# A first load of y on ScalarE's DMA queue, issued beside SyncE's first load of x

## The chip, the cores and the metric

The kernel runs on one core of one Trainium2 chip. The metric is the time of one execution on the device, in microseconds (us), lower is better. Ratios are the mean time of one kernel's runs over that of the other's in the same rounds, so they are not quite the ratio of the medians quoted beside them. Each series of experiments ran beside the kernel before on a chip of its own. The span is the part of an execution that the profile shows; it is 1.4 to 1.9 us shorter than the time. A packet is here one record of a DMA engine, one contiguous run of bytes; a transfer lands when its semaphore shows that all of it has arrived.

## The reference

```python
x, y: float32 [1024, 4096]
z = x + y
out = 0.5 * z * (1 + tanh(sqrt(2 / pi) * (z + 0.044715 * z**3)))   # float32
```

So 2 x 16.78 MB are read and 16.78 MB are written: 50.33 MB.

## The kernel before

Each of the 128 partitions holds 32,768 columns, in 16 chunks of 2,048. x is loaded in two transfers (16,384 columns, 65,536 B a partition), y in four (y0 to y3, 32,768 B a partition) into two buffers, and the result leaves in three stores. SyncE issues all of them on its one queue.

```python
    xloads = [16384, 16384]
    yloads = [8192, 8192, 8192, 8192]
    FIRST = 8
    stores = [16384, 10240, 6144]
...
    by_dve = {0: 0, 2: 0, 4: 2, 6: 4, 8: 8, 12: 10}   # add of chunk k by VectorE, ahead of its end(value)
...
    def add(c):      # z = x + y: VectorE for the chunks in by_dve, GpSimd for the other ten
        eng = nc.vector if c in by_dve else nc.gpsimd
        eng.tensor_add(out=zt[:, a:b], in0=zt[:, a:b], in1=yt[s][:, o : o + b - a])
    def mag(c):      # ScalarE: w = |z|, into PSUM
        nc.scalar.activation(out=wt[c], in_=zt[:, a:b], func=act.Abs)
    def gelu(c):     # ScalarE: w = gelu(-w), in PSUM
        nc.scalar.activation(out=wt[c], in_=wt[c], func=act.Gelu_apprx_tanh, scale=-1.0)
    def end(c):      # VectorE: z = max(z, 0) + w   (chunk 8, FIRST, in two halves)
        nc.vector.scalar_tensor_tensor(out=zt[..], in0=zt[..], scalar=0.0,
                                       in1=wt[c][..], op0=alu.max, op1=alu.add)
...
    # SyncE's queue: x(0), y0, y1, x(1), y2, y3, then the three stores;
    # y2 waits until y0's buffer is free; the first store waits for chunk FIRST
```

After compilation `begin_early(nc, 2)` moves SyncE's first two issues (x and y0) ahead of the barrier at which all engines start (1.26 us for ScalarE's table load in the timeline below). (The last function, `wait_late`, leaves the wait for the last store to ScalarE at the very end, and isn't touched.)

## Time and profile before

| | before |
|---|---|
| time, median of 3 runs (lowest to highest) | 120.17 us (120.11 to 120.28) |
| span of the profiled run | 118.8 us |
| busy: VectorE, ScalarE, GpSimd | 50%, 51%, 47% |
| the DMA queue's packets, share of 16 engines | 98.5% |
| mean rate over the span | 424 GB/s |

The way to read it: a share of half for each compute engine and of nearly all for the DMA engines says where the bound is, and the rate with the compute engines idle (437 GB/s from 3 to 15 us) and busy (437 GB/s from 31.6 to 70 us) says whether the transfers slow down when they work. The prediction below shows the lines. One pair of rows of GpSimd in the timeline (columns: start, length, engine, line, operation, shapes, and in brackets the idle time before it and what ended that) becomes important later. It is that of its first two adds of the second half:

```profile
70.53 6.62 POOL L149 TENSOR_TENSOR z<-z,y 128x2048 f32<-128x2048 f32 x1 [14.56 <-DMA y<-in_y_dram]
...
77.10 4.52 POOL L149 TENSOR_TENSOR z<-z,y 128x2048 f32<-128x2048 f32 x1
```

The same add takes 4.52 us once and 6.62 us once. The longer one began less than 0.05 us after an add of VectorE that took 2.29 us (its row stands in the prediction, at 70.48).

### The profile page before, as it was taken

The numbers are of one execution on the slowest core, as the hardware profiler recorded it, in microseconds if no ns is written. First come the engines' busy times: TensorE is split into PE (matmuls) and PEld (weight loads), VectorE is DVE, ScalarE is ACT, GpSimd is POOL, SyncE is SP. The second block draws the span as 40 slices with busy tenths as digits, with TensorE's granted clock in tenths as the row PEclk, the third lists the DMA queues.
The fourth block names the chain that finished last, engine by engine and source line by source line (L and its number), as shares of the span: only waits on it lengthen the run. The fifth ranks groups of instructions, "written<-read, shape, count | busy, mean of one in ns | idle before, by whom it ended". The sixth has DMA issues, their size and how long they took to land.

```text
span 118.8 us, 160 instructions
## 1 busy us (share of the span) xinstructions
DVE 59.8 (50%) x24; ACT 60.8 (51%) x34; POOL 55.5 (47%) x14
## 2 busy tenths in 40 slices
DVE  0000000000399999699994595257999457742000
ACT  5000000000057989999369804797798999940000
POOL 0000000000399999998000029999999999200000
DMA  9899988989999988998899999998899889999895
GB/s 353 353 419 596 397 353 364 497 375 463 419 430 452 530 353 375 640 397 353 353 463 419 452 430 397 474 541 353 375 640 397 353 353 441 441 441 441 381 422 257
DMA packets 1296, 50.33 MB, mean 424 GB/s; under 512 B 144, under 2 KB 144, under 8 KB 144
## 3 DMA queue, kind: packets, MB, share of 16 engines
q1 hardware_dynamic: 1296, 50.33, 98.5%
HBM read 33.55 MB, written 16.78 MB: 424 GB/s over the span
## 4 chain that ended last, share of the span: by engine, by line
DMA 48%; POOL 33%; POOLq 4%; ACT 3%; DVE 2%; issue 0%; SPq 0%; DVEq 0%
DMA y<-in_y_dram 48%; POOL z L149 33%; POOLq L215 4%; DVE z L166 2%; ACT w L154 2%; ACT w L157 2%; SPq L125 0%; POOLq L149 0%; DVEq L166 0%
## 5 line engine op out<-in xcount | busy, mean ns | idle before, releaser
L149 POOL TENSOR_TENSOR z<-z,y 128x2048 f32<-128x2048 f32 x10 | 55.3, 5560 | 45.9 <-DMA y<-in_y_dram 45.9
L154 ACT ACTIVATE w<-z 128x2048 f32<-128x2048 f32 x16 | 30.1, 1880 | 42.8 <-DVE z L149 36.3
L166 DVE SCALAR_TENSOR_TENSOR z<-z,w 128x2048 f32<-128x2048 f32 (+1 forms) x17 | 36.3, 2156 | 16.0 <-ACT w L157 16.0
L149 DVE TENSOR_TENSOR z<-z,y 128x2048 f32<-128x2048 f32 x6 | 24.0, 4009 | 30.6 <-DMA y<-in_y_dram 30.6
L157 ACT ACTIVATE w<-w 128x2048 f32<-128x2048 f32 x16 | 29.8, 1862 | 0.5
L200 ACT ACT_TABLE_LOAD x1 | 1.3, 1283 | 1.3 <-PEq L232 1.3
L199 DVE MEMSET one<- 128x1 f32 x1 | 0.1, 59 | 1.3 <-PEq L232 1.3
L200 ACT ACTIVATE one<-one 128x1 f32<-128x1 f32 x1 | 0.2, 203 | 0.0
L232 POOL MEMSET const-float32-0.0<- 128x1 f32 x1 | 0.1, 99 | 0.2 <-issue 0.2
L232 POOL MEMSET const-bfloat16-1.0<- 128x1 bf16 x1 | 0.1, 102 | 0.0
L232 POOL MEMSET const-uint8-127<- 128x1 uint8 x1 | 0.1, 102 | 0.0
L232 POOL MEMSET const-float32-1.0<- 128x1 f32 x1 | 0.1, 99 | 0.0
## 6 DMA issues: line engine op xcount, KB each, us to landing
y<-in_y_dram SPq DMA_DIRECT2D x4, 4096.0 KB, 28.3
out_dram<-z SPq DMA_DIRECT2D x1, 5120.0 KB, 14.9
out_dram<-z SPq DMA_DIRECT2D x1, 3072.0 KB, 10.9
z<-in_x_dram SPq DMA_DIRECT2D x2, 40.5
out_dram<-z SPq DMA_DIRECT2D x1, 21.6
```

What stands on the lines that cost most here:

```text
L149: eng.tensor_add(out=zt[:, a:b], in0=zt[:, a:b], in1=yt[s][:, o : o + b - a])
L154: nc.scalar.activation(out=wt[c], in_=zt[:, a:b], func=act.Abs)
L157: nc.scalar.activation(out=wt[c], in_=wt[c], func=act.Gelu_apprx_tanh, scale=-1.0)
L166: ins = nc.vector.scalar_tensor_tensor(out=zt[:, a + o : a + o + n], in0=zt[:, a + o : a + o + n], scalar=0.0, in1=wt[c][:, o : o + n], op ...
L199: nc.vector.memset(one, 0.0)
L200: nc.scalar.activation(out=one, in_=one, func=act.Gelu_apprx_tanh)
L215: tc.compile()
L232: nc = _bacc.Bacc("TRN2", target_bir_lowering=False, num_devices=1)
```

## The change

The intent: y0 need not stand behind x in SyncE's queue. ScalarE has a queue of its own and nothing to do at the start (its first row in the timeline before, the table load, comes at 1.26 us), so it issues y0 as its very first instruction, while SyncE issues x.

```diff
-def begin_early(nc, count):
+def begin_early(nc):
     head, body = (b.instructions for b in nc.main_func.blocks[:2])
-    SP = mybir.EngineType.SP
-    moved = [i for i in body if i.engine == SP and isinstance(i, mybir.InstDMACopy)][:count]
-    ...
+    for engine in (mybir.EngineType.SP, mybir.EngineType.Activation):
+        first = next(
+            i for i in body if i.engine == engine and isinstance(i, mybir.InstDMACopy)
+        )
+        ...
+        body.remove(first)
+        head.insert(next(k for k, i in enumerate(head) if i.engine == engine), first)
...
-        nc.sync.dma_start(out=yt[s][:, o : o + b - a], in_=yv[:, a:b])
+        eng = nc.sync if i else nc.scalar
+        eng.dma_start(out=yt[s][:, o : o + b - a], in_=yv[:, a:b])
...
-    begin_early(nc, 2)
+    begin_early(nc)
```

More of the change, by code (lines that the diff above doesn't have):

```diff
@@ L6 @@
 from concourse._compat import with_exitstack
-def begin_early(nc, count):
+def begin_early(nc):
     head, body = (b.instructions for b in nc.main_func.blocks[:2])
-    SP = mybir.EngineType.SP
-    moved = [i for i in body if i.engine == SP and isinstance(i, mybir.InstDMACopy)][:count]
-    assert not any(i.sync_info and i.sync_info.on_wait for i in moved)
-    assert all(i.regs_accessed() == ((), ()) for i in moved)
-    at = next(k for k, i in enumerate(head) if i.engine == SP)
-    for k, i in enumerate(moved):
-        body.remove(i)
-        head.insert(at + k, i)
+    for engine in (mybir.EngineType.SP, mybir.EngineType.Activation):
+        first = next(
+            i for i in body if i.engine == engine and isinstance(i, mybir.InstDMACopy)
+        )
+        assert not (first.sync_info and first.sync_info.on_wait)
+        assert first.regs_accessed() == ((), ())
+        body.remove(first)
+        head.insert(next(k for k, i in enumerate(head) if i.engine == engine), first)
 def wait_late(nc):
```

## The prediction

> **What bounds the kernel now.** I read the page's head first, then its DMA part, then windows of the trace, then SyncE's timeline. The page:
>
> ```profile
> span 118.8 us, 160 instructions
> ...
> DVE 59.8 (50%) x24; ACT 60.8 (51%) x34; POOL 55.5 (47%) x14
> ...
> DMA packets 1296, 50.33 MB, mean 424 GB/s; under 512 B 144, under 2 KB 144, under 8 KB 144
> ...
> q1 hardware_dynamic: 1296, 50.33, 98.5%
> ```
>
> No compute engine is busy much more than half of the span, but the one DMA queue's packets fill 98.5% of the time of 16 DMA engines. Is that a full rate, or slow packets? The windows view (columns: stretch, length, busy DVE, ACT and POOL, clock, DMA share, GB/s) answers:
>
> ```profile
> 3.00:15.00 12.00, 0.00 (x0) 0.00 (x0) 0.00 (x0) 1.00 1.01 437
> 31.60:70.00 38.40, 34.19 (x12) 29.57 (x16) 24.22 (x4) 1.00 1.01 437
> 85.00:105.00 20.00, 14.50 (x6) 18.57 (x11) 16.59 (x4) 1.00 0.97 422
> ```
>
> The rate is the same with idle compute engines (3 to 15) and busy ones (31.6 to 70). A packet counts where it starts, so such a window is good to some per cent. Sharper: in the trace's packet records a 65,536 B packet takes 2.418 us at the median, and each engine starts its next packet as the last one ends, with no gap over 0.06 us from its first packet to its last. So 16 engines move 16 x 65,536 / 2.418 = 433.7 GB/s, and 50.33 MB need 50,330 / 433.7 = **116.05 us** at the least. The span of 118.8 leaves 2.75 us that is not steady streaming, and only that can shrink. Where it lies, at the front:
>
> ```profile
> 0.00 0.38 SPq L125 DMA_DIRECT2D z<-in_x_dram  x1
> 0.23 0.10 POOL L232 MEMSET const-float32-0.0<- 128x1 f32 x1 [0.23 <-issue]
> ...
> 0.43 1.16 SPq L132 DMA_DIRECT2D y<-in_y_dram  x2
> 1.26 1.28 ACT L200 ACT_TABLE_LOAD   x1 [1.26 <-PEq L232]
> ```
>
> SyncE's first issue (x, columns 0 to 16383) is over at 0.38; the second (y0) starts at 0.43, so the new version can advance y0 by about 0.4 us and no more. The third (y1, merged into the same row) comes after the starting barrier. The packet records have the first data packet at 1.01 us, the sixteenth engine's first at 1.52 us, and those first packets last 2.6 to 3.5 us in place of 2.42. At the end the last packet is over at 118.34 and the last semaphore comes at 118.75. The engine that began at 1.15 us with a 3.50 us packet sums up well: 1.15 + (3.50 - 2.42) + 116.05 + 0.4 = 118.7.
>
> The page's chain of waits names compute after the loads (POOL 33%), but that is a chain of releases; the stores' issue times show its slack:
>
> ```profile
> 77.86 0.35 SPq L136 DMA_DIRECT2D out_dram<-z  x1
> ...
> 96.59 0.34 SPq L136 DMA_DIRECT2D out_dram<-z  x1
> ...
> 107.81 0.33 SPq L136 DMA_DIRECT2D out_dram<-z  x1
> ```
>
> The last y load lands at 80.1 (semaphore records), the first store at 99.4, the second at 111.5. An issue takes 1.0 us to its first packet (as at the front), and a landing shows some 0.4 us after its last packet (as at the end). So a store may come 1.4 us before the earlier landing without a gap: the three stores have 0.8, 1.4 and 2.3 us to spare on the engine that is last. Compute isn't the bound, but has only about 1 us in hand at the first store.
>
> [...]
>
> **The change part by part.** The bytes, tiles, sums and stores stay as they are. A comparison of the instruction order confirms that SyncE loses one DMA issue, ScalarE gains one ahead of everything else, and VectorE and GpSimd keep their order.
> - *Removed:* 0.42 us of SyncE's queue. Work waits on the DMA engines, which have about 19 us of x ahead of them, not on the issue. Gain: 0.
> - *Barrier earlier:* it needs SyncE, now free at about 0.4 us in place of 0.85; ScalarE's own issue of about 0.4 us takes that up in part. The table load and y1's issue come perhaps 0.3 us earlier; ScalarE's first real work is at 34.0 us, y1's data at about 31. Gain: 0.
> - *Moved:* x and y0 now share the engines from 1 us on. The first sum needs both, that is 8.39 + 4.19 = 12.58 MB in either order: 12,580 / 433.7 = 29.0 us plus the start, the 31.6 at which y0 lands now. x should land near 31 in place of 21.9 and nothing asks for it sooner. Gain: 0.
> - *First packet:* x is issued as before, so 1.01 us stays. An engine whose first x packet comes late (1.52) might start on y0's first. I choose a gain of 0.1 us out of the 0.5 us spread, a guess.
> - *Tail:* the same stores on the same queue. 0.
>
> Sum: 120.17 - 0.1 = **120.07**, written 120.1.
>
> **The rivals.**
> 1. *Overlapped queues shorten the start.* First packets take about 0.7 us more than steady ones; if that is latency of one queue's first read, a second queue could fill it. For: the excess is there. Against: both begin at the same moment, and neither is warm. It would make 119.4. One in eight.
> 2. *Switching costs.* Each engine turns between 8 packets of x and 8 of y0, some 16 switches. With 0.05 us lost in each, 0.8 us are added, and all of it reaches the end, as the engines have no slack: 121.0. To pass 2% (2.4 us), 0.15 us a switch is needed. Against: in the old trace neighbouring packets join without gaps even where x ends and y0 begins; but that is one queue. One in eight, beyond 2% one in thirty.
> 3. *y1 slips in front of y0's end.* y1 now stands behind x on SyncE's queue, not behind y0. If y0 lags by a packet, one y1 packet (1.21 us) goes first, y0 lands at 32.8 and VectorE's eight chunks finish that much later. Two rows of the old timeline carry the slack:
>
> ```profile
> 67.91 2.29 DVE L166 SCALAR_TENSOR_TENSOR z<-z,w 128x2048 f32<-128x2048 f32 x1 [1.46 <-ACT w L157]
> 70.48 2.29 DVE L149 TENSOR_TENSOR z<-z,y 128x2048 f32<-128x2048 f32 x1 [0.29 <-DMA y<-in_y_dram]
> ```
>
> VectorE ends its first half at 70.20 and waits 0.29 us for y2. Of 1.2 us, 0.3 vanish there and 0.8 in the first store's slack, so about 0.1 us is left: 120.2. Likely in part (one in three), and almost free.
> 4. *The issue holds x up.* [...] One in six.
>
> **Range and chances.** Most ways end between 119.9 and 120.5, the rivals at 119.4 and 121.0. The range 119.5 to 120.9 leaves one in ten on either side. Faster by 2% would be 117.8; without any start or end cost the span would be 116.05 and the time, 1.4 us longer than the span as now, 117.4. Almost all of the overhead would have to go: 1%. Slower by 2% needs rival 2 at its strongest: 3%. The rest, 96%, is within.
>
> **What would show it.** In the new profile: two data queues, together again near 98.5%; x landing at about 31 us, within 2 us of y0; the first VectorE sum at 31.3 to 32.9; stores at about 78, 96.6 and 107.8; 65,536 B packets alone at 2.42 us after the first load. If x lands near 22 and y0 near 31, the queues don't share. If the first sum starts after 33 us while y1 has not gained, switching costs. If the first packet comes before 0.9 us, the start is shortened, and rival 1 or an earlier ScalarE did it. The prediction is wrong if the steady packet time changes while two queues run, or if a gap of over 0.5 us opens ahead of the first store.

The fourth rival: by the length of one issue (0.38 us for x, 0.42 for y0), that rival put x up to 0.4 us late, at 120.5. That the steady part has nothing to give rests on the rate alone (437 GB/s with compute idle and busy, packets of 2.418 us without gaps); that no faster packets are possible is the assumption. That the engines take turns between two queues, which "Moved" and the second and third rival build on, was at that time an assumption as well; the packet records of the changed kernel show it, below.

## The result, and the profile after

The changed kernel took 120.30 us (median of 6 runs, 120.15 to 120.52), the kernel before 120.22 us (6 runs). The ratio is 1.0007, with a 95% interval of 0.9995 to 1.002: the same.

The page of the changed kernel has two data queues where there was one:

```profile
span 119.0 us, 160 instructions
...
DMA packets 1296, 50.33 MB, mean 423 GB/s; under 512 B 144, under 2 KB 144, under 8 KB 144
...
q1 hardware_dynamic: 1152, 46.14, 90.6%
q10 hardware_dynamic: 144, 4.19, 8.2%
```

Together they fill 98.8% of the engines' time: as full as before, with the same packets and bytes. The start of the timeline:

```profile
0.00 0.39 SPq L125 DMA_DIRECT2D z<-in_x_dram  x1
0.12 0.37 ACTq L133 DMA_DIRECT2D y<-in_y_dram  x1
...
0.91 1.28 ACT L201 ACT_TABLE_LOAD   x1 [0.91 <-PEq L233]
0.91 0.33 SPq L133 DMA_DIRECT2D y<-in_y_dram  x1
```

ScalarE issues y0 at 0.12 us, 0.31 us earlier than SyncE did, and does so while SyncE issues x; neither takes longer than alone (0.39 us for x and 0.37 for y0, against 0.38 and 0.42 one after the other in the kernel before). The barrier is over 0.35 us sooner (the table load begins at 0.91 in place of 1.26). Then nothing follows from it. The packet records show the first packet of x at 1.02 us and the first of y0 at 3.93 us: each engine first finishes a packet of x. The landings show what was traded:

| landing, us | before | changed | changed, second trace |
|---|---|---|---|
| x, first load | 21.91 | 31.60 | 31.56 |
| y0 | 31.61 | 31.76 | 31.74 |
| y1 | 41.33 | 41.33 | 41.29 |
| y2 | 70.39 | 70.63 | 70.35 |
| last store | 118.75 | 119.00 | 118.71 |

x lands 9.7 us later and y0 within 0.15 us of where it did. As the first sum needs both, it starts within 0.16 us of where it did (31.70 before):

```profile
31.86 2.29 DVE L150 TENSOR_TENSOR z<-z,y 128x2048 f32<-128x2048 f32 x1 [30.82 <-DMA y<-in_y_dram]
31.90 6.61 POOL L150 TENSOR_TENSOR z<-z,y 128x2048 f32<-128x2048 f32 x1 [31.46 <-DMA y<-in_y_dram]
...
68.06 2.29 DVE L167 SCALAR_TENSOR_TENSOR z<-z,w 128x2048 f32<-128x2048 f32 x1 [1.46 <-ACT w L158]
70.72 2.29 DVE L150 TENSOR_TENSOR z<-z,y 128x2048 f32<-128x2048 f32 x1 [0.37 <-DMA y<-in_y_dram]
```

The last two rows answer to the two that the prediction shows under its third rival. The first store is issued at 78.10 (77.86 before). The profiled run was the slowest of the six; the 0.2 us by which its later times lag are absent in the second trace.

### The profile page after: what moved, and what is told of

It reads as the page before. It is cut to its first block, busy times and chain, and to the rows that moved or that the text cites. A ratio compares the mean times of both kernels' runs of the same rounds, so it can differ in the third digit from the quotient of the medians.

```text
span 119.0 us, 160 instructions
## 1 busy us (share of the span) xinstructions
DVE 59.8 (50%) x24; ACT 60.8 (51%) x34; POOL 55.5 (47%) x14
## 4 chain that ended last, share of the span: by engine, by line
DMA 48%; POOL 33%; POOLq 4%; ACT 3%; DVE 2%; issue 0%; DVEq 0%
DMA y<-in_y_dram 48%; POOL z L150 33%; POOLq L216 4%; DVE z L167 2%; ACT w L155 2%; ACT w L158 2%; POOLq L150 0%; DVEq L167 0%
## 6 DMA issues: line engine op xcount, KB each, us to landing
y<-in_y_dram ACTq DMA_DIRECT2D x1, 4096.0 KB, 31.6
```

## The experiments

There were eleven more runs, one of them of the changed kernel as it is; all gave correct results. The kernel before ran beside them in the same rounds (120.19 to 120.27 us).

### What each part of the change is worth

**The changed kernel again**, unedited, with more rounds.

> The changed kernel again, for a closer ratio and a second trace. Theory (only the first data packet's moment and the 434 GB/s of the engines count, and the change moves neither): ratio 0.999 to 1.001, y0 and x landing within 0.5 us of each other at 31.4 to 31.8. Rival (taking turns between two queues costs some ns at each of 16 switches): ratio 1.001 to 1.003 again, y0 landing at 31.7 or later, as in the first trace.

Measured: 120.26 us (5 runs), ratio 0.9997, interval 0.9984 to 1.0011. x and y0 landed 0.18 us apart. The first comparison's 1.0007 was within the noise; a switching cost visible in the time is not there. One sign of the rival's did come, y0 landing after 31.7, but not for its reason: the last packet of y0 ended at 31.25 us in the kernel before and at 31.23 and 31.18 in the two traces of the changed one. Only the landing came later after it, 0.53 to 0.57 us in place of 0.35; why stays open.

**y0 issued by SyncE, but after the barrier.** An edit of the kernel before:

```diff
-    begin_early(nc, 2)
+    begin_early(nc, 1)
```

> The kernel before with y0 still on SyncE's queue, but issued after the starting barrier, some 0.5 us later than before. Theory (the engines have about 19 us of x to move first, so the moment of y0's issue is worth nothing): ratio 0.999 to 1.001, y0 landing at 31.6 as before. Rival (issuing y0 early is worth its 0.4 us): 120.6, ratio 1.003 to 1.004.

Measured: 120.33 us, ratio 1.0003 (0.9990 to 1.0016). y0 was issued at 0.78 us and landed at 31.66, 0.05 us from before. Between 0.12 us (ScalarE's queue), 0.43 and 0.78 us (SyncE's) the moment at which y0 is issued is worth nothing. A later one is another matter, as shown below.

**Both loads after the barrier.** An edit of the changed kernel:

```diff
-    begin_early(nc)
     wait_late(nc)
```

> The changed kernel, but neither load is moved ahead of the barrier: x is issued some 0.5 to 0.7 us later, y0 from ScalarE at about 2 us. Theory (the first packet's moment is fully exposed): the whole delay of x comes through, 120.6 to 120.9, ratio 1.003 to 1.006. Rival (the start is hidden behind something else): 120.2, ratio under 1.001.

Measured: 120.90 us, ratio 1.0052 (1.0039 to 1.0064). Its timeline:

```profile
0.74 0.38 SPq L125 DMA_DIRECT2D z<-in_x_dram  x1
0.81 0.06 DVE L200 MEMSET one<- 128x1 f32 x1 [0.81 <-PEq L232]
0.91 0.36 ACTq L133 DMA_DIRECT2D y<-in_y_dram  x1
```

x is issued 0.74 us after the span's start, in place of 0.00. The two traces have the same start: GpSimd's first memset comes at 0.24 us here and at 0.23 before. The first packet comes at 1.74 us in place of 1.01, so x is 0.73 us later, and the time grew by 0.63 us (by the interval of the ratio, 0.47 to 0.77): within the noise, all of the delay comes through. (y0 came at 0.91, sooner than the 2 us expected, as ScalarE's sequencer issued it during the table load, which ran from 0.73 to 2.01.) This is the front that is exposed: the first load's issue, not the second's.

### How two queues share an engine

The pair of runs cuts x's first load and y0 into runs of 4,096 B, with 128 packets of x and 64 of y0 on each engine in place of 8 and 8. Control and test differ in y0's queue, and so in what goes ahead of the starting barrier (in the control both halves of x, in the test the first half of x and of y0).

```diff
+    def pieces(ap, half):
+        return ap.rearrange("p (i j e) -> p i j e", j=2, e=1024)[:, :, half]
...
+        for half in (0, 1) if i == 0 else ():
+            nc.scalar.dma_start(out=pieces(t, half), in_=pieces(yv[:, a:b], half))   # control: nc.sync
```

> The kernel before with x's first load and y0 each cut into two issues of 4,096 B runs, so that each engine has 128 packets of x and 64 of y0, all on SyncE's queue: the control for the run with two queues. x lands near 22, y0 near 31.7; 120.2 to 120.8, depending on what small packets cost by themselves.

> The changed kernel with the same 4,096 B runs, x on SyncE's queue and y0 on ScalarE's: some 128 switches between queues on each engine in place of 16. Theory (turns are taken packet by packet and a switch costs nothing): y0 lands at 21 to 22 and x at 31 to 32 (64 packets of each go first), and the time is within 0.1% of the control. Rival (a switch costs 10 ns or more): at least 1.3 us slower than the control. [...]

Measured: 121.87 us for one queue (ratio to the kernel before 1.0136), 121.94 us for two (1.0142). The difference of 0.07 us over 128 switches an engine, with intervals of 0.0015 on each ratio, excludes 10 ns a switch. The median 4,096 B packet took 162 ns on SyncE's queue in both, and 160.5 ns on ScalarE's. So switching costs nothing that these runs can see.

The control, 1.4% over the kernel before, was slower than expected: 162 ns a packet is 404 GB/s, against 434 for the large ones. (In it x landed at 22.9 us and y0 at 33.2.) The landings with two queues were missed too: y0 24.4 us, not 21 to 22, and x 33.3, not 31 to 32. The packet records explain it: y0's first packet came at 2.85 us, some ten packets of x (1.7 us) after y0 could have begun by the 1.0 us from issue to first packet seen for x (an estimate; why it came later stays open), and from there 64 packets of each queue took 20.9 us up to 23.76, that is 128 x 162 ns. The turns are taken packet by packet, one for one, at the sizes tried here (65,536 with 32,768 B, and 4,096 with 4,096 B). That is why x and y0 land together in the changed kernel: 8 packets each, in turns. The pair shows one more thing: y1's issue on SyncE, 0.33 us in the changed kernel, took 5.07 us in the control and 16.90 us in the run with two queues, where it stands behind small runs; no run tests why.

### What a late y0 costs

The third rival says that a y0 late by a packet is almost free. The edit of the changed kernel leaves y0 on ScalarE and holds it back with tiny activations:

```diff
-    for engine in (mybir.EngineType.SP, mybir.EngineType.Activation):
+    for engine in (mybir.EngineType.SP,):
...
+        for _ in range(LATE):      # 40, then 2
+            nc.scalar.activation(out=one, in_=one, func=act.Gelu_apprx_tanh)
```

**LATE = 40:**

> The changed kernel with y0 on ScalarE's queue held back by 40 tiny activations, to about 12 us, so that x runs ahead and y1 shares the engines with the end of y0. Theory (turns packet by packet, and about 1.1 us of slack in all before the first store): x lands near 25, y0 near 36 to 37, about 5 us later than before, the first store is issued about 4.8 us later, a gap of about 4 us opens on the DMA engines ahead of the stores, and the time is 123.5 to 124.7. Rival (the transfers are the bound and any delay of the sums is hidden): 120.2 to 120.6.

Measured: 128.50 us, ratio 1.0683 (1.0669 to 1.0698). The direction was as the theory had it, the size twice as large. y0 was issued at 11.46 us; its first packet came at 16.06, five turns of x (2.42 us each) after 3.93; x landed at 25.4, y0 at 37.6, 6.0 us late. VectorE's first half ended 6.0 us late as well (76.16 in place of 70.20). But the first store came 8.8 us late (86.62). The missing 2.8 us are in one instruction:

```profile
76.08 5.45 DVE L151 TENSOR_TENSOR z<-z,y 128x2048 f32<-128x2048 f32 x1
```

VectorE's add of chunk 8 took 5.45 us in place of 2.29, 3.2 us more; some 0.4 us came back, as the wait for y2 ahead of it fell away. It began at 76.08, while GpSimd was in an add of its own that ended at 79.39, and it ended 2.15 us after that.

That made a new theory: **an add of VectorE that meets one of GpSimd under way waits until it ends.** Then a small lateness is a cliff. The add above agrees, with its end 2.15 us after GpSimd's. So do three adds in the trace of the kernel before: they began at 33.91, 52.50 and 83.26 us, while GpSimd was in an add, took 6.59, 5.62 and 4.98 us, and each ended 2.15 us after it. It bears on the two pairs of rows above: in the kernel before VectorE starts just under 0.05 us ahead of GpSimd, and there GpSimd's add is the longer one, by 2.1 us of its 6.62, while VectorE, on whose chunk 8 the first store waits, takes its 2.29. What makes the two hold each other up, no run here shows.

**LATE = 2:**

> The changed kernel with y0's issue held back by 2 tiny activations, to about 2.5 us, so that y0 misses one turn or two on each engine and one or two packets of y1 go ahead of its last. From the run held back to 11.5 us: y0 landed 6.0 us late for 5 missed turns, so 1.2 us a turn. Theory of a cliff (an add of VectorE that meets an add of GpSimd under way waits until it ends): y0 lands at 32.8 to 34.2, VectorE's first half ends 1.2 to 2.4 us later than 70.2, its add for chunk 8 then begins behind GpSimd's first add of the second half and ends near 77.2 in place of 72.8, the first store is issued at about 82.3, and the time is 123.5 to 124.5. Rival (the prediction's third rival: 0.3 us of wait and 0.8 us of slack absorb all but a part): 120.2 for one turn, 121.5 for two.

Measured: 124.33 us, ratio 1.0338 (1.0323 to 1.0353). y0 landed at 33.7, 2.0 us late: 14 of the 16 engines missed one turn and two of them missed two. VectorE, GpSimd and SyncE in this run's timeline:

```profile
70.02 2.29 DVE L168 SCALAR_TENSOR_TENSOR z<-z,w 128x2048 f32<-128x2048 f32 x1 [1.46 <-ACT w L159]
70.68 4.50 POOL L151 TENSOR_TENSOR z<-z,y 128x2048 f32<-128x2048 f32 x1 [12.61 <-DMA y<-in_y_dram]
72.22 5.11 DVE L151 TENSOR_TENSOR z<-z,y 128x2048 f32<-128x2048 f32 x1
...
82.42 0.35 SPq L138 DMA_DIRECT2D out_dram<-z  x1
```

y2 lands as always and GpSimd starts at once, at 70.68; VectorE comes at 72.22, waits inside its add (the row shows no wait for a semaphore) for GpSimd's end at 75.18, and ends at 77.33, 2.15 us later (72.77 before). The store follows 4.56 us late.

**The same, with VectorE's add of chunk 8 put ahead of its last step for chunk 7:**

```diff
-    by_dve = {0: 0, 2: 0, 4: 2, 6: 4, 8: 8, 12: 10}
+    by_dve = {0: 0, 2: 0, 4: 2, 6: 4, 8: 7, 12: 10}
```

> The same with VectorE's add for chunk 8 put ahead of its last step for chunk 7, so that it waits for y2 and starts together with GpSimd. Theory of the cliff: chunk 8's add ends near 72.8 again although y0 is just as late, the first store is issued by 78.5, and the time is 120.2 to 120.8. Rival (the lateness of y0 itself is what costs): as slow as the run without this edit, within 0.5 us.

Measured: 120.63 us, ratio 1.0031 (1.0014 to 1.0047). y0 landed at 33.6, just as late, and 3.7 of the 4.1 us are gone:

```profile
70.62 2.29 DVE L151 TENSOR_TENSOR z<-z,y 128x2048 f32<-128x2048 f32 x1 [2.23 <-DMA y<-in_y_dram]
70.66 6.63 POOL L151 TENSOR_TENSOR z<-z,y 128x2048 f32<-128x2048 f32 x1 [12.74 <-DMA y<-in_y_dram]
72.83 2.28 DVE L168 SCALAR_TENSOR_TENSOR z<-z,w 128x2048 f32<-128x2048 f32 x1
...
78.01 0.35 SPq L138 DMA_DIRECT2D out_dram<-z  x1
```

VectorE now waits 2.23 us for y2 with the add in hand, and starts ahead of GpSimd. Lateness by itself isn't what costs. The 0.36 us that stay are hardly in the span (118.7 to 118.9 us in the four runs, as in the kernel before): they lie in the part of the time outside it, 1.8 to 1.9 us in place of 1.5; why stays open.

### The cliff without a late load

To take the loads out of it, tiny memsets were put on VectorE in the kernel before, between its last step for chunk 7 and its add of chunk 8:

```diff
+    def pad(c):
+        for _ in range(PAD):       # 1, then 8
+            nc.vector.memset(scrap, 0.0)      # 128x1
...
+        dve += [(pad, c)] if c == 8 else []
         dve += [(add, k) for k in sorted(by_dve) if by_dve[k] == c] + [(end, c)]
```

> The kernel before with 1 memset of 128x1 (some 0.06 us) on VectorE between its last step for chunk 7 and its add for chunk 8. Theory of the cliff: VectorE has 0.19 us in hand before y2 lands there, so chunk 8's add still starts together with GpSimd's and lasts 2.29 us: 120.2 to 120.4. Rival (extra work on VectorE costs its own length): the same, so this run alone tells nothing apart; it is the near side of the next.

> The same with 8 such memsets (0.5 to 1.0 us in all); loads are as before, y0 is not late. Theory of the cliff: VectorE comes to chunk 8's add at 70.7 to 71.2, after GpSimd began its own at 70.5, waits for that to end near 75.0, ends its add near 77.3 in place of 72.8, and the first store is issued at about 82.3: 123.6 to 124.4. Rival (extra work on VectorE costs at most its own length, less the slack): 120.2 to 120.8.

Measured: with one memset 120.29 us, ratio 1.0010 (0.9995 to 1.0025); with eight 124.28 us, ratio 1.0339 (1.0322 to 1.0357). The timeline with one memset, then with eight:

```profile
70.02 0.06 DVE L154 MEMSET scrap<- 128x1 f32 x1
70.36 2.29 DVE L150 TENSOR_TENSOR z<-z,y 128x2048 f32<-128x2048 f32 x1 [0.28 <-DMA y<-in_y_dram]
70.40 6.61 POOL L150 TENSOR_TENSOR z<-z,y 128x2048 f32<-128x2048 f32 x1 [14.56 <-DMA y<-in_y_dram]
...
77.74 0.35 SPq L137 DMA_DIRECT2D out_dram<-z  x1
```

```profile
69.98 0.94 DVE L154 MEMSET scrap<- 128x1 f32 x8
70.39 4.49 POOL L150 TENSOR_TENSOR z<-z,y 128x2048 f32<-128x2048 f32 x1 [14.58 <-DMA y<-in_y_dram]
70.91 6.12 DVE L150 TENSOR_TENSOR z<-z,y 128x2048 f32<-128x2048 f32 x1
...
82.12 0.35 SPq L137 DMA_DIRECT2D out_dram<-z  x1
```

0.94 us of memsets turn the order of two adds round: GpSimd's falls from 6.61 to 4.49 us and VectorE's grows from 2.29 to 6.12. How this reaches the end is to be seen in the DMA engines' own row, from 79 to 84 us in 40 slices of 0.125 us (a packet shows in the slice in which it starts), first with one memset, then with eight:

```profile
DMA  0999900000000000000099999000000000000000
```

```profile
DMA  0000000000000000000000000000000990000000
```

With one memset the first store's packets begin on the heels of the last load, at 79.1 to 79.6, and again one packet later. With eight, nothing starts until 82.96. The engines that are the bound stand idle for over 3 us.

**The changed kernel with this order of adds**, and no delay:

> The changed kernel with VectorE's add for chunk 8 put ahead of its last step for chunk 7, without a delay of y0. Theory: where nothing is late the order change costs nothing and gains nothing, as the DMA engines are the bound: ratio 0.998 to 1.002, first store at 77.8 to 78.3. Rival (the last step for chunk 7, 2.3 us later, holds up ScalarE's buffers): over 120.6.

Measured: 120.28 us, ratio 1.0008 (0.9993 to 1.0023), first store at 78.01. The order costs nothing here. No run beat either kernel, and the experiments point to none that would by much: 116.05 us of the 118.8 are steady streaming.

## Why the prediction was right or wrong

The time (120.1, range 119.5 to 120.9) held. Point by point:

- *The bound and its floor:* held. The 65,536 B packets have the same 2.418 us at the median while two queues run, and the two queues' shares add up to 98.8%.
- *Removed issue, earlier barrier, moved packets, each worth 0:* held in sum, by the ratio of 0.9997. That the moment of y0's issue is worth nothing is shown by the run with 0.78 us and 1.0003; the other two were not tested apart. x landed at 31.6 where "near 31" was said.
- *First packet, the guessed gain of 0.1 us:* wrong. The step said that an engine whose first x packet comes late might start on y0's. No engine did: the first y0 packets came at 3.93 to 4.66 us. The term is 0, and the ratio of the second series, 0.9997, has no room to show 0.1 us (0.0008) either way.
- *Rival 1, a shorter start:* ruled out in its premise, as y0's packets come only after x's first.
- *Rival 2, switching costs:* ruled out, by the pair with 128 switches.
- *Rival 4, the issue holds x up:* ruled out: 0.39 us for x beside 0.37 us for y0, first packet at 1.02 (before: 0.38 us for x alone, first packet at 1.01).
- *Rival 3, y1 slips in front:* it didn't happen in the changed kernel, as y0 was queued in time for the second turn, so its error didn't reach the forecast. In that the number was lucky: the prediction gave the slip one in three, and the run in which VectorE came half a microsecond late took 124.28 us, outside the range. For its size was wrong by far. The step "Of 1.2 us, 0.3 vanish there and 0.8 in the first store's slack, so about 0.1 us is left" took the delay to pass through VectorE's add unchanged. By its reckoning the 2.0 us of the run with LATE = 2 leave 0.9 us; measured were 4.1. The term left out is the wait behind GpSimd's add: 5.11 us for an add of 2.29, that is 2.8 more; with it the reckoning gives 3.7, and the span grew by 3.9. The other two terms hold: in that run VectorE's first half ended 2.1 us late and its add began 1.7 us late, so some 0.4 us vanished in the wait for y2; with eight memsets the store was 4.3 us late and the span 3.6 us longer, so about 0.7 us of slack was used, where 0.8 was said. (The time grew by 4.1 us in both runs; the rest is again outside the span.) The old profile had shown the missing term:

```profile
L149 DVE TENSOR_TENSOR z<-z,y 128x2048 f32<-128x2048 f32 x6 | 24.0, 4009 | 30.6 <-DMA y<-in_y_dram 30.6
```

VectorE's six adds last 4.01 us on average, and a free one 2.29. Three of them took 4.98 to 6.59 us, because they came second: each began while GpSimd was in an add and ended 2.15 us after it.

The row "0.29 <-DMA y<-in_y_dram" was thus read as slack of 0.29 us. It is also the whole distance to a cliff: a VectorE that comes half a microsecond later loses the race for the add and about 4 us with it. No run of either kernel here has a time that would show it over the edge.

## What to carry to other kernels

In these runs, where the DMA engines stream without gaps, a second queue added no transfer time and took none (ratio 0.9997): it re-dealt which bytes come first, packet for packet (x landed at 31.60 us in place of 21.91). So it pays only if something can start on what comes earlier, and here the first sum needs both loads. At the front only the issue of the very first load was exposed (0.73 us later, 0.63 us longer). And where one engine's instruction waits for the whole of another's, as VectorE's add did behind GpSimd's (5.11 to 6.12 us in place of 2.29), read a small idle gap ahead of the pair as the margin of a race, and put the instruction that the critical path needs first in its queue, so that it wins.
